# Differential attention: squares of the output rows ahead of two casts, and the third transposes of a step behind six products

## The chip, the core and the metric

The kernel runs on one core of a Trainium2 chip. What is measured is the device time of one execution in microseconds (us). Three runs of the kernel before have a median of 2905.68 us (2904.09 to 2906.51). The engines are named as in the profile: PE is the matrix engine (PEld its weight loads, which run beside its matmuls), DVE the vector engine, ACT the scalar (activation) engine, POOL the general engine, SP the engine that issues most DMAs (transfers between memory and the chip).

## What is computed

One layer of a hybrid model for two streams, a prompt of 256 tokens and 2048 latent tokens. The part that the change touches is differential attention with four heads: two softmax maps are formed from the same keys, the second is subtracted with a factor, and the result is multiplied with the values and normalised per row.

```python
def diff_attention(q, k, v, lam):
    ...
        s = jnp.einsum('bqhmd,bkhmd->bhmqk', qblk, k).astype(jnp.float32) * scale
        p = jax.nn.softmax(s, axis=-1)
        a = p[:, :, 0] - lam * p[:, :, 1]
        return jnp.einsum('bhqk,bkhe->bqhe', a.astype(v.dtype), v)
...
def merge(attn, four, subln_g, lam_init, w_out):
    b, n = attn.shape[:2]
    a = rms_norm(attn, subln_g) * (1.0 - lam_init)
    return jnp.concatenate([a.reshape(b, n, ATTN_WIDTH), four], axis=-1) @ w_out
```

The latent queries attend to 512 cached and 2048 new keys, 2560 in all. Projections, a Fourier mixing, the output projection and an MLP stand before and behind the attention; the change leaves them as they are.

## The kernel before

**Tiles.** For each of the 4 heads the 2048 latent queries are cut into 8 groups of 256, which makes 32 groups. A group has two halves j of 128 queries and two maps m. For each (j, m) there are five score blocks of 128 queries by 512 keys (`fill`, L1081, two matmuls each), a row maximum per block on DVE (`rowmax`, L1086), a combination of the five maxima (`comb`, L1089), and five exponentials on ACT (`exp`, L1105) that write the tile P0 (m = 0) or P1 (m = 1). POOL then forms P0 plus factor times P1 (`combine`, L1112 to L1121).

The 2560 keys are 20 tiles of 128, taken in pairs kb = 0, 2, ..., 18. For a pair, PE transposes four 128x128 pieces of P0 into one PSUM bank (`tr`, L1136, tile `pts`), ACT casts that bank into a high part (`ah`, L1143, tile `ahs`), DVE subtracts to get the low part (`al`, L1148, tile `als`), and PE multiplies both tiles of the pair with the values in three products each (`mul`, through `mm3`, L95 to L97). Pair 4 stays one whole fp32 copy and is multiplied by L1162. Pair 14 (tiles 14 and 15), like all the others, is split into two parts.

**PSUM.** It has eight banks: five for scores, two for `pts`, and one, `po`, which all groups share. In `po` columns 0 to 255 gather the products of a group. Columns 256 to 511 hold the finished group's output after it is transposed back (`o2`, L1177), from which ACT takes the squares and their row sums (`o4`, L1183, tile `osqs`). The `pts` banks alternate, so the transposes of a pair wait until `al` of the pair before the last one has read its bank.

**Order.** The attention's order is written out by hand: each call is entered with a due time in a list, which is then sorted, and each engine runs its share of that list in order. T is one step, u a fifth of it. A group's keys take four steps, with the pairs (0, 2), (4, 6, 8), (10, 12) and (14, 16, 18). A step also holds the scores, maxima and exponentials of a later group. In this document the four steps are called:

- **A**: transposes of 10 and 12, products of 4, 6, 8. The squares of the preceding group stand here.
- **B**: transposes of 14, 16, 18, products of 10 and 12.
- **C**: transposes of the next group's 0 and 2, products of 14, 16, 18.
- **D**: transposes of 4, 6, 8, products of 0 and 2. The preceding group's `o2` stands here.

In step A of a group, ACT's list reads: five exponentials into P0, the casts of 10 and 12, the two squares of the group before, then five exponentials into P1. PE's list reads: transposes of 10, three score blocks, transposes of 12, two score blocks, L1162 (pair 4), products of 6 and 8. In four of a head's eight cycles PE also has two small matmuls of the prompt stream (L1221) behind the products of step B, and in one cycle the prompt's products (L1256) in the middle of B.

The due times that the change edits, with w the start of a step (L1345) and, in L1355, of the output part of a group:

```python
tr_t, ah_t, al_t = [0.7, 2.2, 3.86], [3.2 if q == 3 else 3.3, 3.8, 4.4], [3.22 if q == 3 else None, 4.6, 5.2]
...
add(w + T + (3.9 + 0.01 * n) * u, gr.mul, kb)
...
for t, fn in ((0, gr.o1), (0.4, gr.o2), (7.85, gr.o4), (9.2, gr.o5), (11.8, gr.o6), (16.3, gr.o7), (23.4, gr.o8), (26.0, gr.o9)):
```

## Time and profile before

| what | us |
|---|---|
| median of three runs | 2905.68 |
| the profiled execution | 2906.36 |
| its span, first to last instruction | 2904.6 |
| PE busy | 2833.2 |
| DVE busy | 1995.9 |
| ACT busy | 1538.4 |
| POOL busy | 1073.8 |

The profile holds one execution. The attention runs from about 545 to 1292 us of the span. Read the whole first, then the stage: PE is busy for 98% of the span, but inside the attention less, and there DVE, ACT and POOL are each busy for four fifths of the time or more. In a row of the timeline stand the start in us, the duration in us (for merged rows the whole run of them), the engine, the line, the operation, the tile written and the tiles read, shapes, the count, and in brackets the idle time before it with what ended that. Ends of PE's matmuls are modelled. PE's granted clock is full in the attention.

### The profile page before, as it was taken

Reading aid. Unit: us, or ns where it says so; the run is one execution under the profiler, and the core shown is the slowest. Engines: PE = TensorE matmul, PEld = TensorE weight load, DVE = VectorE, ACT = ScalarE, POOL = GpSimd, SP = SyncE. Lnnn points to the kernel's source line nnn. Section 1 sums busy time; section 2 is a strip of 40 time slices with the busy share of each in tenths; the row PEclk is TensorE's granted clock in tenths of the full one; section 3 lists DMA queues with packets and bytes.
Section 4 is the critical chain, followed back from the end, with each engine's and each line's share of the span. In section 5 each row is a group of like instructions: output and inputs, shape, how many; then the busy total and the mean of one; then the engine's idle time right before and its main releaser. Section 6 shows DMA issues by size and latency. Waiting matters only on the chain.

```text
span 2904.6 us, 43029 instructions
## 1 busy us (share of the span) xinstructions
PE 2833.2 (98%) x15029; PEld 2441.0 (84%) x15029; DVE 1995.9 (69%) x3357; ACT 1538.4 (53%) x3479; POOL 1073.8 (37%) x887
## 2 busy tenths in 40 slices
PE   8999999999999999989999999999999999999999
PEld 5888888677777777778889999999998888888887
DVE  7767786888887888874468778777775354345554
ACT  4333333888888888863346556556554332232221
POOL 1211124788888888862213333333332000000000
PEclk9999999999999999999999999999999999999999
DMA  7776767332222321336786667676656454445663
GB/s 280 222 205 203 228 204 252 140 108 45 77 72 52 108 43 43 95 68 194 229 260 212 223 231 240 223 240 222 220 192 243 149 188 153 137 145 179 205 212 109
DMA packets 403707, 497.17 MB, mean 171 GB/s; under 512 B 31475, under 2 KB 319584, under 8 KB 400418
## 3 DMA queue, kind: packets, MB, share of 16 engines
q1 hardware_dynamic: 398000, 483.83, 52.7%
q0 software_dynamic: 1936, 7.41, 0.8%
q10 hardware_dynamic: 3554, 3.17, 0.3%
q8 instruction: 119, 1.95, 0.3%
q14 instruction: 98, 0.80, 0.1%
HBM read 316.78 MB, written 179.62 MB: 171 GB/s over the span
## 4 chain that ended last, share of the span: by engine, by line
PE 53%; DVE 1%; DMA 1%; ACT 0%; issue 0%; SPq 0%; POOL 0%; DVEq 0%
PE ps L95 8%; PE ps L97 8%; PE ps L96 8%; PE pC L1759 2%; PE pB L1760 2%; PE pB L1759 2%; PE pC L1761 2%; PE pC L1760 2%; PE pB L1761 2%; PE pA L1760 2%; PE pA L1761 2%; PE pA L1759 2%; PE po L97 2%; PE po L95 2%; PE po L96 2%; PE pD L1761 1%
## 5 line engine op out<-in xcount | busy, mean ns | idle before, releaser
L1086 DVE TENSOR_REDUCE mxs<-Ss 128x1 f32<-128x512 f32 x636 | 407.7, 685 | 123.6 <-PE Ss L1081 114.2
L1436 DVE TENSOR_TENSOR sl<-sr,sh 128x768 fp32r<-128x768 f32 x168 | 161.8, 964 | 331.5 <-ACT sh L1435 331.0
L1121 POOL TENSOR_TENSOR P0s<-P0s,P1s 128x1024 f32<-128x1024 f32 (+2 forms) x128 | 376.6, 2942 | 10.7
L1435 ACT CAST sh<-sr 128x768 fp32r<-128x768 f32 x168 | 140.6, 838 | 418.2 <-PE ps L96 418.2
L1801 POOL TENSOR_TENSOR gs<-g,g 128x384 f32<-128x384 f32 x48 | 69.8, 1453 | 469.6 <-ACT g L1771 426.4
L1105 ACT ACTIVATE P1s<-Ss,mxs 128x512 f32<-128x512 f32 x318 | 215.5, 694 | 35.4 <-DVE mxs L1089 34.1
L95 PE MATMUL pj<-wh,hh 128*128 128x512 f32 x576 | 228.3, 396 | 2.8 <-DVE hh L556 2.0
L96 PE MATMUL pj<-wl,hh 128*128 128x512 f32 x576 | 227.1, 394 | 0.5 <-DVE wl L517 0.5
L95 PE MATMUL ps<-thT,sh 128*128 128x512 f32 x585 | 227.6, 389 | 0.0
L96 PE MATMUL ps<-tlT,sh 128*128 128x512 f32 x585 | 227.6, 389 | 0.0
L97 PE MATMUL ps<-thT,sl 128*128 128x512 f32 x585 | 227.6, 389 | 0.0
L97 PE MATMUL pj<-wh,hl 128*128 128x512 f32 x576 | 225.5, 392 | 0.0
L1105 ACT ACTIVATE P0s<-Ss,mxs 128x512 f32<-128x512 f32 x318 | 214.6, 692 | 4.9 <-DVE mxs L1089 4.0
L1143 ACT CAST ahs<-pts 128x512 fp32r<-128x512 f32 x288 | 165.5, 607 | 81.5 <-PE pts L1136 81.4
L1136 PE MATMUL pts<-ident,P0s 128*128 128x128 f32 x1280 | 192.8, 274 | 15.1 <-DVE als L1148 11.8
L1136 PEld LDWEIGHTS pts<-ident,P0s 128*128 128x128 f32 x1280 | 148.6, 140 | 55.8 <-PE Ss L1081 25.7
L1148 DVE TENSOR_TENSOR als<-pts,ahs 128x512 fp32r<-128x512 f32 x288 | 185.3, 681 | 10.8 <-ACT ahs L1143 10.6
L1081 PE MATMUL Ss<-KS1s,Qs 128*128 128x512 f32 x636 | 190.1, 422 | 2.1 <-ACT P0s L1105 2.1
L1081 PE MATMUL Ss<-KS0s,Qs 128*128 128x512 f32 x636 | 189.3, 418 | 0.4 <-ACT P1s L1105 0.4
L1770 ACT ACTIVATE g<-uz 128x384 f32<-128x384 f32 x144 | 75.7, 526 | 200.2 <-DVE uz L1793 174.1
L1120 POOL TENSOR_SCALAR P1s<-P1s,tots 128x1024 f32<-128x1024 f32 (+2 forms) x128 | 172.0, 1344 | 5.7
L95 PE MATMUL po<-ahs,Vs 128*128 128x256 f32 x576 | 172.3, 299 | 0.0
(530 smaller groups left out, 8003.9 us busy)
## 6 DMA issues: line engine op xcount, KB each, us to landing
sr<-sd SPq DMA_DIRECT2D x84, 768.0 KB, 4.5
a<-in_w SPq DMA_DIRECT2D x184, 256.0 KB, 3.9
sd<-gs SPq DMA_DIRECT2D x192, 192.0 KB, 2.0
sd<-g SPq DMA_DIRECT2D x144, 192.0 KB, 2.0
wm<-in_w_mod SPq DMA_DIRECT2D x32, 512.0 KB, 5.6
Qs<-qd SPq DMA_DIRECT2D x32, 512.0 KB, 5.9
b<-in_w SPq DMA_DIRECT2D x64, 256.0 KB, 4.8
b<-tsum SPq DMA_DIRECT2D x64, 256.0 KB, 4.8
```

Of the source, the lines that this page charges most:

```text
L95: nc.tensor.matmul(ps, lh, rh, start=first, stop=False)
L96: nc.tensor.matmul(ps, lh, rl, start=False, stop=False)
L97: nc.tensor.matmul(ps, ll, rh, start=False, stop=last)
L1081: nc.tensor.matmul(S[:, :w], self.Q[:, x, m, j * P:j * P + P], self.hd.KS[m][:, b * 512:b * 512 + w], start=(x == 0), stop=(x == 1))
L1086: nc.vector.tensor_reduce(self.mx[j][:, m, b:b + 1], self.S[j, m, b], axis=AX.X, op=ALU.max)
L1105: nc.scalar.activation(dst, S, AF.Exp, bias=self.mx[j][:, m, 6:7], accum_out=self.sm[j][:, m, b:b + 1])
L1121: nc.gpsimd.tensor_add(d, d, p)
L1136: nc.tensor.transpose(pt[:, c:c + P], self.p0[j][:, (kb + t) * P:(kb + t + 1) * P], ident)
L1148: nc.vector.tensor_sub(t, self.pt[kb], f32(self.A[kb][0]))
L1759: nc.tensor.matmul(ps, wh[:, c], hh[:, k, :], start=first and k == 0, stop=False, skip_group_check=True)
L1760: nc.tensor.matmul(ps, wh[:, c], hl[:, k, :], start=False, stop=False, skip_group_check=True)
L1761: nc.tensor.matmul(ps, wl[:, c], hh[:, k, :], start=False, stop=k == 3, skip_group_check=True)
```

## The change

Two due times differ.

```diff
-                            tr_t, ah_t, al_t = [0.7, 2.2, 3.86], [3.2 if q == 3 else 3.3, 3.8, 4.4], [3.22 if q == 3 else None, 4.6, 5.2]
+                            tr_t, ah_t, al_t = [0.7, 2.2, 3.905 if q == 3 else 3.86], [3.2 if q == 3 else 3.3, 3.8, 4.4], [3.22 if q == 3 else None, 4.6, 5.2]
...
-                    for t, fn in ((0, gr.o1), (0.4, gr.o2), (7.85, gr.o4), (9.2, gr.o5), (11.8, gr.o6), (16.3, gr.o7), (23.4, gr.o8), (26.0, gr.o9)):
+                    for t, fn in ((0, gr.o1), (0.4, gr.o2), (6.9, gr.o4), (9.2, gr.o5), (11.8, gr.o6), (16.3, gr.o7), (23.4, gr.o8), (26.0, gr.o9)):
```

The later edit in the code is the earlier in the cycle. On ACT in step A (here group 1 casts its pairs 10 and 12, group 3 has its exponentials, and the squares `osqs_0` are of group 0) the order before is:

```order
L1105 ACTIVATE P0s_3_0_5905,sms_3_0_5844<-Ss_3_0_0_4_5877,mxs_3_0_5843 128x512
L1143 CAST ahs_1_10_5950<-pts_1_10_5913 128x512
L1143 CAST ahs_1_12_5955<-pts_1_12_5939 128x512
L1183 ACTIVATE osqs_0_5957,osss_0_5958<-po 128x128 x2
L1105 ACTIVATE P1s_3_0_0_5979,sms_3_0_5844<-Ss_3_0_1_0_5918,mxs_3_0_5843 128x512
```

And on ACT at the same place after the change:

```order
L1105 ACTIVATE P0s_3_0_5905,sms_3_0_5844<-Ss_3_0_0_4_5877,mxs_3_0_5843 128x512
L1183 ACTIVATE osqs_0_5949,osss_0_5950<-po 128x128 x2
L1143 CAST ahs_1_10_5954<-pts_1_10_5913 128x512
L1143 CAST ahs_1_12_5959<-pts_1_12_5939 128x512
L1105 ACTIVATE P1s_3_0_0_5979,sms_3_0_5844<-Ss_3_0_1_0_5918,mxs_3_0_5843 128x512
```

The two squares have moved ahead of the two casts; the number of instructions is the same.

The other edit is on PE in step B, shown here for group 1 (`pts_1_16`, `pts_1_18` are its transposes, `po` its products). Before:

```order
L1081 MATMUL Ss_3_1_0_4_6024<-KS0s_5257,Qs_3_5621 128x512 x2
L1136 MATMUL pts_1_18_6029<-ident,P0s_1_0_5425 128x128
L1136 MATMUL pts_1_18_6029<-ident,P0s_1_1_5493 128x128
L1136 MATMUL pts_1_18_6029<-ident,P0s_1_0_5425 128x128
L1136 MATMUL pts_1_18_6029<-ident,P0s_1_1_5493 128x128
L95 MATMUL po<-ahs_1_10_5950,Vs_5315 128x256
L96 MATMUL po<-als_1_10_5977,Vs_5315 128x256
L97 MATMUL po<-ahs_1_10_5950,Vs_5315 128x256
L95 MATMUL po<-ahs_1_10_5950,Vs_5315 128x256
L96 MATMUL po<-als_1_10_5977,Vs_5315 128x256
L97 MATMUL po<-ahs_1_10_5950,Vs_5315 128x256
L95 MATMUL po<-ahs_1_12_5955,Vs_5315 128x256
```

On PE at the same place after the change:

```order
L1081 MATMUL Ss_3_1_0_4_6024<-KS0s_5257,Qs_3_5621 128x512 x2
L95 MATMUL po<-ahs_1_10_5954,Vs_5315 128x256
L96 MATMUL po<-als_1_10_5977,Vs_5315 128x256
L97 MATMUL po<-ahs_1_10_5954,Vs_5315 128x256
L95 MATMUL po<-ahs_1_10_5954,Vs_5315 128x256
L96 MATMUL po<-als_1_10_5977,Vs_5315 128x256
L97 MATMUL po<-ahs_1_10_5954,Vs_5315 128x256
L1136 MATMUL pts_1_18_6036<-ident,P0s_1_0_5425 128x128
L1136 MATMUL pts_1_18_6036<-ident,P0s_1_1_5493 128x128
L1136 MATMUL pts_1_18_6036<-ident,P0s_1_0_5425 128x128
L1136 MATMUL pts_1_18_6036<-ident,P0s_1_1_5493 128x128
L95 MATMUL po<-ahs_1_12_5959,Vs_5315 128x256
```

The four transposes of pair 18 have moved behind the six products of pair 10. Both edits stand once in each of the 32 groups, except that the squares of the last group have a place of their own behind the loop, which stays. On DVE and POOL no row moves. On SP one store of an output tile (`att`, L1208) changes places with one load of input rows (L1576) at the end of the attention.

## The prediction

> **What bounds the kernel now.** First the page, then the windows, then the list of waits. Over the span PE is the bound; in the attention it is not full.

> ```profile
> PE 2833.2 (98%) x15029; PEld 2441.0 (84%) x15029; DVE 1995.9 (69%) x3357; ACT 1538.4 (53%) x3479; POOL 1073.8 (37%) x887
> ```
> ```profile
> 560.00:1250.00 690.00, 653.13 (x4143) 536.42 (x4141) 564.78 (x1104) 586.04 (x1634) 596.00 (x472) 1.00 0.26 69
> ```

> In these 690 us PE is busy for 653.13 at the full granted clock (1.00), so 36.9 us are to be had there. The list of waits (engine, line, releaser: total us, times, longest) names two rows that hold nearly all of it:

> ```profile
> PE po L1162 <- ACT osqs L1183: 28.2, 31, 1.4
> PE pts L1136 <- DVE als L1148: 11.8, 27, 1.8
> ```

> The reader is to see that each edit aims at one of them. L1162 waits for the squares once in each cycle; the third transposes wait for a subtraction.

> I read one cycle engine by engine, steps A to C. PE:

> ```profile
> 724.39 1.18 PE L1081 MATMUL Ss<-KS1s,Qs 128*128 128x512 f32 x4
> 726.43 1.13 PE L1162 MATMUL po<-ahs,vf4s 128*128 128x256 f32 x4 [0.86 <-ACT osqs L1183]
> ...
> 728.82 0.60 PE L1136 MATMUL pts<-ident,P0s 128*128 128x128 f32 x4
> 729.17 1.63 PE L1081 MATMUL Ss<-KS0s,Qs 128*128 128x512 f32 x6
> 730.64 0.60 PE L1136 MATMUL pts<-ident,P0s 128*128 128x128 f32 x4
> 730.99 1.18 PE L1081 MATMUL Ss<-KS0s,Qs 128*128 128x512 f32 x4
> 732.55 0.63 PE L1136 MATMUL pts<-ident,P0s 128*128 128x128 f32 x4 [0.38 <-DVE als L1148]
> ...
> 733.26 0.28 PE L97 MATMUL po<-ahs,Vs 128*128 128x256 f32 x1
> ...
> 733.94 0.28 PE L97 MATMUL po<-ahs,Vs 128*128 128x256 f32 x1
> ...
> 734.54 0.63 PE L1136 MATMUL pts<-ident,P0s 128*128 128x128 f32 x4
> ```

> A cycle later L1162 starts and waits in the same way, 23.6 us on:

> ```profile
> 750.03 1.13 PE L1162 MATMUL po<-ahs,vf4s 128*128 128x256 f32 x4 [0.87 <-ACT osqs L1183]
> ```

> The stretch of ACT around the first of these two:

> ```profile
> 723.96 0.70 ACT L1105 ACTIVATE P0s<-Ss,mxs 128x512 f32<-128x512 f32 x1
> 724.53 0.22 ACT L1105 ACTIVATION_READ_ACCUMULATOR P0s<-Ss,mxs 128x1 f32 x1
> 724.62 1.09 ACT L1143 CAST ahs<-pts 128x512 fp32r<-128x512 f32 x2
> 725.57 0.32 ACT L1183 ACTIVATE osqs<-po 128x128 f32<-128x128 f32 x1
> ...
> 726.01 0.28 ACT L1183 ACTIVATE osqs<-po 128x128 f32<-128x128 f32 x1
> 726.19 0.19 ACT L1183 ACTIVATION_READ_ACCUMULATOR osqs<-po 128x1 f32 x1
> 726.71 0.69 ACT L1105 ACTIVATE P1s<-Ss,mxs 128x512 f32<-128x512 f32 x1 [0.33 <-DVE mxs L1089]
> ```

> **Edit 1, the squares first.** It adds no instruction. The squares start at 725.57 because two casts from 724.62 stand ahead; without these they start 0.95 earlier. L1162 starts 0.42 behind the second square's start (726.43 against 726.01), so its release moves to 725.06 + 0.42 = 725.48. When could PE use it? Its scores end at 724.39 + 1.18 = 725.57 as modelled, but work behind a score run starts 0.16 before that modelled end (730.64 against 729.17 + 1.63 = 730.80), so at 725.41. The release still comes last, by 0.07, and the gain is 726.43 - 725.48 = **0.95 us a cycle**. The other bound is the counted idle, 0.86; I take the first, since it is the time by which the late releaser moves.

> What is behind the moved work? The casts of 10 and 12 come later by the squares' 0.86 (two starts 0.44 apart, and as much again before the next instruction can go). Their readers, and those of step B, on DVE:

> ```profile
> 726.54 1.28 DVE L1148 TENSOR_TENSOR als<-pts,ahs 128x512 fp32r<-128x512 f32 x2
> 729.92 1.89 DVE L1086 TENSOR_REDUCE mxs<-Ss 128x1 f32<-128x512 f32 x3 [2.11 <-PE Ss L1081]
> 731.73 0.68 DVE L1148 TENSOR_TENSOR als<-pts,ahs 128x512 fp32r<-128x512 f32 x1
> ...
> 733.63 0.16 DVE L1089 TENSOR_REDUCE mxs<-mxs 128x1 f32<-128x5 f32 x1
> 733.71 1.28 DVE L1148 TENSOR_TENSOR als<-pts,ahs 128x512 fp32r<-128x512 f32 x2
> ```

> Cast 10 now ends near 724.62 + 0.86 + 0.60 = 726.08, before its subtraction at 726.54; cast 12 ends near 726.55, before its own at about 727.14. ACT waits 0.33 for the maxima ahead of 726.71, and the squares and casts together are as long as before, so the exponentials into P1 do not move. In B, DVE idles 2.11 us for PE's scores, so it follows PE by the full 0.95. Its first subtraction then comes at 730.78 and needs the cast of 14, whose row, with the later ones of ACT, is here:

> ```profile
> 730.04 0.60 ACT L1143 CAST ahs<-pts 128x512 fp32r<-128x512 f32 x1
> ...
> 733.22 0.59 ACT L1143 CAST ahs<-pts 128x512 fp32r<-128x512 f32 x1 [1.36 <-PE pts L1136]
> ...
> 733.83 0.69 ACT L1105 ACTIVATE P0s<-Ss,mxs 128x512 f32<-128x512 f32 x1
> ...
> 735.37 0.34 POOL L1112 TENSOR_SCALAR tots<-tots,nlam 128x1 f32<-128x1 f32 x1 [2.10 <-ACT P0s L1105]
> ...
> 736.00 0.30 PEld L1081 LDWEIGHTS Ss<-KS1s,Qs 128*128 128x128 f32 x2 [0.34 <-ACT P0s L1105]
> ```

> That cast ends at 730.64: a margin of 0.14, the narrowest of the cycle. POOL idles 2.10 before C and keeps over 1 us.

> There are 31 such waits. 29 are of this kind: 29 x 0.95 = 27.6 us. The last two, at the end, are longer:

> ```profile
> 1268.73 1.03 PE L1136 MATMUL pts<-ident,P0s 128*128 128x128 f32 x8
> 1271.21 1.13 PE L1162 MATMUL po<-ahs,vf4s 128*128 128x256 f32 x4 [1.45 <-ACT osqs L1183]
> ...
> 1284.76 1.13 PE L1162 MATMUL po<-ahs,vf4s 128*128 128x256 f32 x4 [1.40 <-ACT osqs L1183]
> ```

> There no exponentials stand directly ahead, and the squares can run while PE transposes 10 and 12. I take both waits whole: 2.8 us. **Edit 1: -30.4 us.**

> [...] The squares read columns 256 to 511 of `po` and L1162 writes columns 0 to 255: no byte in common, yet the row above shows 0.86 us of waiting. [...] Guarding by address would make the releaser in the list a wrong one, and edit 1 worth nothing.

> **Edit 2, the third transposes behind six products.** In B the scores could hand over at 730.99 + 1.18 - 0.16 = 732.01; the transposes start at 732.55, 0.14 after the subtraction that frees their bank (731.73 + 0.68). Six products fill that gap: the rows at 733.26 and 733.94 lie six products apart, 0.68, so 0.70 with the start. The transposes then start at 732.71, 0.16 later than now, of which 0.02 to 0.03 return because they no longer stall between the first two (0.60 long, not 0.63). I take **0.14 later**.

> Does PE get its 0.38 back? The next bank is wanted at 734.54 for the transposes of step C, and that start stands 0.15 behind the second subtraction (733.71 + 0.68 = 734.39), which hangs on DVE's maxima and not on this order. So PE reaches it half a microsecond early and waits there: the wait moves, the step keeps its length.

> Who waits for the third cast? ACT idles 1.36 for it; it ends at 733.81 and the exponential starts at 733.83, when the maxima (733.63 + 0.16) are done too: both arrive together. 0.14 on the cast is 0.14 on the exponentials of C, and the weight load of the third score block there already waited 0.34 for them (736.00). From there PE has no idle until A that could absorb it. So edit 2 **costs** 0.14 in each of 27 cycles, 3.8 us. In one cycle per head the prompt's products stand in B and the transposes come later anyhow:

> ```profile
> 1064.84 1.18 PE L1081 MATMUL Ss<-KS0s,Qs 128*128 128x512 f32 x4
> 1066.12 0.63 PE L1136 MATMUL pts<-ident,P0s 128*128 128x128 f32 x4
> ```

> Scores hand over at 1065.86, plus 0.70 is 1066.56, against 1066.12: 0.44, less 0.03, in four cycles: 1.6 us. **Edit 2: +5.4 us**, between -11.8 (all of the wait in the list is saved) and +22 (31 x 0.70, the products whole); the rows above are nearest.

> The swap on SP puts a 512 KB load ahead of a store at the end of the attention. A load of that size, and PE behind that place:

> ```profile
> Qs<-qd SPq DMA_DIRECT2D x32, 512.0 KB, 5.9
> ```
> ```profile
> 1300.00:1400.00 100.00, 99.40 (x471) 82.70 (x470) 52.35 (x78) 33.90 (x84) 22.32 (x24) 1.00 0.72 213
> ```

> One landing, 5.9 us, bounds it on either side; with PE at 99.4% it is hidden, and I take nothing.

> **Sum** against the profiled execution of 2906.36 us: -30.4 + 5.4 = -25.0, so **2881.4**. That execution lies 0.7 above the median of the runs, within their spread.

> **The rivals.**

> - Edit 2 is free or a gain. For it: the wait is in the list, and 16 of the cycles have prompt matmuls ahead of the next bank, which take up some of the earliness. Against: cast and maxima end together. From 2876 (cost nothing) to 2870 (half of the 11.8 saved). 10%.
> - The next wait takes over. In B the margin of 0.14 between the cast of 14 and its subtraction decides: if squares and casts in the new order push the exponentials into P1 by more than that, DVE, the second subtraction and the next bank slip. 0.3 to 0.4 a cycle gives back 9 to 12: 2890 to 2893. Against it: 0.33 of idle on ACT. 11%.
> - Squares behind an exponential start late. The only idle behind a square is the 0.33 before the exponential; if it were a cost of changing function and fell due at the squares, edit 1 loses 29 x 0.33 = 9.6: 2891. 3%. [...]
> - Slower, and the change not doing what it says. If L1162 is held by something else that came just before the squares, edit 1 is worth nothing and edit 2's later cast is left: 2906.4 + 5.4 = 2912, up to 2928. It decides as soon as edit 1 gives less than 5.4 / 31 = 0.17 a cycle. Against it: without the two long ones the waits are (28.2 - 2.85) / 29 = 0.87 each, as even as a fixed order behind the squares would make them. 4%.

> **How the numbers follow.** Forecast 72%, rivals 10, 11, 3 and 4%. The range runs from 2873, where edit 2 is free with a little of its wait saved, to 2891, where the next wait or the late squares begin to give back. About 0.2% (5.8 us) is what a measurement can tell from no change. All cases but the last are faster by more: faster 0.95, same 0.02, slower 0.03.

> **What would show it.** Edit 1: the wait of L1162 for the squares falls from 28.2 us to below 4, and L1162 starts come 22.7 to 22.9 us apart, not 23.6. Edit 2: the third transposes wait for nothing; the first transposes of C wait some 0.3 to 0.5 for a subtraction instead; ACT idles longer before the third cast; PE's score blocks in C show waits for exponentials. If the cycle is under 22.65, edit 2 was free; if the subtraction of 14 waits for its cast, the margin was the step that failed; if the cycle is still 23.6, edit 1 was.

## The result and the profile after

The changed kernel takes 2876.74 us (median of 4 runs, 2873.97 to 2878.94), the kernel before, run beside it, 2905.02 us. The ratio is 0.9902, with a 95% interval of 0.9885 to 0.9919. The profiled execution took 2876.21 us, its span is 2874.4. The forecast was 2881.4 with a range of 2873 to 2891.

The first part of the page of the changed kernel (engine, busy time, share of the span, instructions), and its windows over the attention without the first and last microseconds (length, busy time of PE, PEld, DVE, ACT and POOL, granted clock, DMA share, GB/s):

```profile
PE 2832.3 (99%) x15029; PEld 2445.7 (85%) x15029; DVE 1995.9 (69%) x3357; ACT 1531.6 (53%) x3479; POOL 1074.6 (37%) x887
```
```profile
560.00:1225.00 665.00, 651.98 (x4146) 540.16 (x4145) 565.97 (x1106) 581.16 (x1638) 597.57 (x473) 1.00 0.28 71
```

PE's work is the same; its idle time in these windows is 13.0 us here and was 36.9. Four rows of the changed kernel's list of waits say what went:

```profile
PE pts L1136 <- DVE als L1148: 10.7, 27, 1.8
PEld po L1162 <- ACT osqs L1183: 10.1, 31, 0.3
PE Ss L1081 <- ACT P0s L1105: 1.9, 5, 1.1
ACT ahs L1143 <- PE pts L1136: 58.0, 71, 2.1
```

PE has no row for L1162 any more (28.2 us before). Only the weight load that runs ahead of it still meets the squares, 0.3 us each, beside other matmuls. The wait for the subtraction L1148 has nearly kept its size (11.8 before). One cycle of the changed kernel shows that it is another wait under the same name; the timelines of PE, ACT and DVE, cut to the lines in question:

```profile
718.54 1.13 PE L1162 MATMUL po<-ahs,vf4s 128*128 128x256 f32 x4
...
724.83 0.60 PE L1136 MATMUL pts<-ident,P0s 128*128 128x128 f32 x4
...
726.65 0.63 PE L1136 MATMUL pts<-ident,P0s 128*128 128x128 f32 x4 [0.51 <-DVE als L1148]
```
```profile
718.12 0.28 ACT L1183 ACTIVATE osqs<-po 128x128 f32<-128x128 f32 x1
...
718.38 1.06 ACT L1143 CAST ahs<-pts 128x512 fp32r<-128x512 f32 x2
719.79 0.69 ACT L1105 ACTIVATE P1s<-Ss,mxs 128x512 f32<-128x512 f32 x1 [0.34 <-DVE mxs L1089]
...
725.46 0.59 ACT L1143 CAST ahs<-pts 128x512 fp32r<-128x512 f32 x1 [1.25 <-PE pts L1136]
725.95 0.69 ACT L1105 ACTIVATE P0s<-Ss,mxs 128x512 f32<-128x512 f32 x1
```
```profile
723.84 0.68 DVE L1148 TENSOR_TENSOR als<-pts,ahs 128x512 fp32r<-128x512 f32 x1
...
725.75 0.16 DVE L1089 TENSOR_REDUCE mxs<-mxs 128x1 f32<-128x5 f32 x1
```

The row at 724.83 is the third transposes of step B: no wait (0.38 before). The row at 726.65 is the first transposes of step C: they now wait 0.51. The other cycles show the same: the first transposes of the next group wait 0.51 to 0.53, or 0.25 to 0.29 where PE comes to them later, mostly because the two small prompt matmuls (L1221) stand ahead (0.41 in the first cycle). L1162 starts 22.56 to 22.63 us apart in the ordinary cycles (those without the prompt's work; one or two stray by 0.3), against 23.54 to 23.60 before. From the first L1162 to the last it is 695.95 us (557.89 to 1253.84), against 725.75: -29.8. Ahead of the first the changed kernel is 1.1 us shorter, which no edit touches (over the twelve profiles of this document the first L1162 lies between 556.3 and 559.7 us). From the start of the last L1162 to the end of the span it is 0.8 us longer (1620.6 against 1619.8). Together that is, but for rounding, the 30.15 us between the two profiled executions.

### The profile page after: what moved, and what is told of

It is laid out like the page before. It is cut to its first block, busy times and chain, and to the rows that moved or that the text cites. A ratio compares the mean times of both kernels' runs of the same rounds, so it can differ in the third digit from the quotient of the medians.

```text
span 2874.4 us, 43052 instructions
## 1 busy us (share of the span) xinstructions
PE 2832.3 (99%) x15029; PEld 2445.7 (85%) x15029; DVE 1995.9 (69%) x3357; ACT 1531.6 (53%) x3479; POOL 1074.6 (37%) x887
## 4 chain that ended last, share of the span: by engine, by line
PE 53%; DVE 1%; DMA 1%; ACT 0%; issue 0%; POOL 0%; DVEq 0%; SPq 0%
PE ps L95 8%; PE ps L96 8%; PE ps L97 8%; PE pB L1761 2%; PE pB L1759 2%; PE pB L1760 2%; PE pC L1759 2%; PE pA L1759 2%; PE pC L1761 2%; PE pA L1761 2%; PE pA L1760 2%; PE pC L1760 2%; PE po L97 2%; PE po L96 2%; PE po L95 2%; PE pD L1759 1%
## 5 line engine op out<-in xcount | busy, mean ns | idle before, releaser
L1086 DVE TENSOR_REDUCE mxs<-Ss 128x1 f32<-128x512 f32 x636 | 407.8, 686 | 97.0 <-PE Ss L1081 85.7
L1105 ACT ACTIVATE P1s<-Ss,mxs 128x512 f32<-128x512 f32 x318 | 215.2, 694 | 36.2 <-DVE mxs L1089 32.8
L97 PE MATMUL ps<-thT,sl 128*128 128x512 f32 x585 | 227.6, 389 | 0.0
L97 PE MATMUL pj<-wh,hl 128*128 128x512 f32 x576 | 225.6, 392 | 0.0
L1105 ACT ACTIVATE P0s<-Ss,mxs 128x512 f32<-128x512 f32 x318 | 214.6, 694 | 4.2 <-DVE mxs L1089 4.0
L1136 PE MATMUL pts<-ident,P0s 128*128 128x128 f32 x1280 | 193.1, 274 | 13.6 <-DVE als L1148 10.7
L1081 PE MATMUL Ss<-KS1s,Qs 128*128 128x512 f32 x636 | 192.9, 425 | 1.9 <-ACT P0s L1105 1.9
L1143 ACT CAST ahs<-pts 128x512 fp32r<-128x512 f32 x288 | 162.7, 606 | 58.3 <-PE pts L1136 58.0
L1148 DVE TENSOR_TENSOR als<-pts,ahs 128x512 fp32r<-128x512 f32 x288 | 185.5, 681 | 8.5 <-ACT ahs L1143 8.4
L1081 PE MATMUL Ss<-KS0s,Qs 128*128 128x512 f32 x636 | 189.6, 418 | 0.4 <-ACT P1s L1105 0.4
L1136 PEld LDWEIGHTS pts<-ident,P0s 128*128 128x128 f32 x1280 | 149.4, 140 | 45.4 <-issue 9.1
## 6 DMA issues: line engine op xcount, KB each, us to landing
wm<-in_w_mod SPq DMA_DIRECT2D x32, 512.0 KB, 5.3
Qs<-qd SPq DMA_DIRECT2D x32, 512.0 KB, 6.3
```

Of the source, the lines that this page charges most:

```text
L97: nc.tensor.matmul(ps, ll, rh, start=False, stop=last)
L1081: nc.tensor.matmul(S[:, :w], self.Q[:, x, m, j * P:j * P + P], self.hd.KS[m][:, b * 512:b * 512 + w], start=(x == 0), stop=(x == 1))
L1086: nc.vector.tensor_reduce(self.mx[j][:, m, b:b + 1], self.S[j, m, b], axis=AX.X, op=ALU.max)
L1105: nc.scalar.activation(dst, S, AF.Exp, bias=self.mx[j][:, m, 6:7], accum_out=self.sm[j][:, m, b:b + 1])
L1136: nc.tensor.transpose(pt[:, c:c + P], self.p0[j][:, (kb + t) * P:(kb + t + 1) * P], ident)
L1148: nc.vector.tensor_sub(t, self.pt[kb], f32(self.A[kb][0]))
```

## Experiments

Two theories of why the change beat its forecast stood at the start: edit 2 costs less than its 5.4 us, or edit 1 gives more than its 30.4. The first two kernels do one edit each. Every ratio is against the kernel before on the same chip.

**Edit 1 alone.**

```diff
-for t, fn in (..., (7.85, gr.o4), ...):
+for t, fn in (..., (6.9, gr.o4), ...):
```

> Edit 1 alone: the squares stand ahead of the casts of 10 and 12, the third transposes stay where they were. Both edits together took 28.3 us off the median (2905.0 to 2876.7). Theory: edit 2 is worth nothing within 1.5 us, because the exponentials of step C follow the maxima and not the third cast; then this runs at 2875 to 2878, L1162 starts 22.6 us apart in most cycles, and the third transposes still wait 0.4 to 0.5 for a subtraction. Rival, the working of the prediction: edit 2 costs 5.4 us, so without it 2871. Second rival: edit 2 saved its wait, so without it 2882 to 2888.

Measured: 2875.78 us (2875.11 to 2879.37; ratio 0.9899, 0.9884 to 0.9914). Ordinary cycles are 22.56 to 22.62, as in the changed kernel, and the third transposes wait as before:

```profile
723.11 0.63 PE L1136 MATMUL pts<-ident,P0s 128*128 128x128 f32 x4 [0.38 <-DVE als L1148]
```

First to last L1162 takes 694.5 us, 31.3 less than before. Edit 1 alone does all that the change does. The first theory held.

**Edit 2 alone.**

```diff
-tr_t, ah_t, al_t = [0.7, 2.2, 3.86], ...
+tr_t, ah_t, al_t = [0.7, 2.2, 3.905 if q == 3 else 3.86], ...
```

> Edit 2 alone: the third transposes stand behind the products of 10, the squares stay behind the casts. Theory (edit 2 worth nothing): 2904 to 2907, cycles of 23.6 us, the wait of L1162 for the squares 28 us as before, the wait for the subtraction moved from the third transposes to the first transposes of the next group. Working of the prediction: 2910. Rival that it saves its wait: 2893 to 2900.

Measured: 2907.5 us (2905.92 to 2909.97; ratio 1.0004, 0.9996 to 1.0013), just above the upper expectation. L1162 waits 28.1 us for the squares, as before. The ordinary cycles are 23.54 to 23.61, unchanged. The four cycles with the prompt's products take 24.85 to 24.89 instead of 24.58 to 24.62. First to last L1162 is 1.6 us longer, 1.1 of it in these four.

**The third transposes behind both pairs of products**, with edit 1. If a later third cast is free at every size, this is free too; if it is free only up to a margin, the rest shows in full.

```diff
-[0.7, 2.2, 3.905 if q == 3 else 3.86]
+[0.7, 2.2, 3.915 if q == 3 else 3.86]
```

> Both edits, but the third transposes behind the products of 10 and of 12, so 0.70 us later still. Theory: the third cast had about no slack left against the maxima (its successor starts 0.1 us before it ends); 0.70 more makes it the last to arrive, the exponentials of C start 0.6 to 0.7 later, and the third score block with them: cycles of 23.2 to 23.3 us, 2893 to 2899. Rival: the exponentials hang on the maxima alone and the third cast is free to move: 2876 to 2878.

Measured: 2899.43 us (2897.59 to 2901.65; ratio 0.9977, 0.9968 to 0.9987), cycles 23.24 to 23.30. ACT and DVE in one of its cycles:

```profile
708.15 0.59 ACT L1143 CAST ahs<-pts 128x512 fp32r<-128x512 f32 x1 [1.89 <-PE pts L1136]
708.63 0.69 ACT L1105 ACTIVATE P0s<-Ss,mxs 128x512 f32<-128x512 f32 x1
```
```profile
707.76 0.16 DVE L1089 TENSOR_REDUCE mxs<-mxs 128x1 f32<-128x5 f32 x1
```

Here the maxima are done at 707.92 and the exponential starts at 708.63: the cast holds it. It starts 0.48 behind the start of the cast, 0.11 before the cast's listed end. In the changed kernel the maxima end at 725.91 and the exponential starts 0.04 behind them, 0.49 behind the start of the cast and 0.10 before its listed end. So in these traces the exponential needs the maxima plus 0.04 and the cast's start plus 0.48. In all twelve profiles no exponential behind a third cast starts earlier than these two, to within 0.01. In the kernel before, cast and exponential started 0.61 apart (733.22 and 733.83): the cast had 0.13 in hand. Edit 2 used that up and, outside the four cycles with the prompt's products, no more. Another 0.7 us of products then cost about 0.68 a cycle.

**The squares between the two casts**, with edit 2: half of edit 1.

```diff
-(7.85, gr.o4)
+(7.6, gr.o4)
```

> Both edits, but the squares between the casts of 10 and 12, half way back. Theory: L1162 is released by the squares, so one cast of 0.47 us ahead of them costs 0.40 to 0.47 a cycle in 29 cycles: cycles of 23.0 to 23.1 us, 2888 to 2891, and a wait of L1162 of 0.3 to 0.4 each. Rival: something that came just before the squares holds L1162: 2877 still. Second rival: any cast ahead brings the whole wait back: 2905.

Measured: 2898.14 us (2891.54 to 2900.33; ratio 0.9968, 0.9956 to 0.998). The cycles came as expected, 23.05 to 23.11, and so did L1162's wait:

```profile
PE po L1162 <- ACT osqs L1183: 13.0, 31, 1.0
```

Each cast ahead of the squares is half a microsecond a cycle. The total is 7 us above the expectation (the five runs lie between 2891.54 and 2900.33). In the profiled execution, 2896.35 us, 5.4 lie behind the last L1162 (1625.2 us to the end of the span, against 1619.8 before); up to 1.7 of that, an estimate of the last section, is a second dip of the granted clock (0.81 and 0.76 in two windows of 4 us from 1289.34). The kernel with the third transposes behind both pairs shows 1624.2 there, edit 1 alone 1622.9. This is where the next three runs look.

**The squares behind the products of 6 and 8**, with edit 2. The order on ACT and on PE is that of edit 2 alone; only who waits for whom changes.

```diff
-(7.85, gr.o4)
+(7.95, gr.o4)
```

> The third transposes as in the change, the squares a little later than in the kernel before, behind the issue of the products of 6 and 8, so that ACT's and PE's orders are those of the kernel with the transposes alone (2907.5), but the squares, which read columns 256 to 511 of po, come behind products that write columns 0 to 255, and the products no longer wait for the squares. No byte is shared. If a bank is guarded as one (what made L1162 wait): the squares wait for the products of 6 and 8, ACT stands until these are through, and exponentials, maxima and scores behind it slip: cycles near 25.4, 2945 to 2965. If guarded by address: no waits either way, the order of ACT as before and PE free of the squares: cycles 22.6 to 22.9, 2876 to 2886.

Measured: 2923.99 us in one run, so without an interval; cycles near 24.33. The list of waits of ACT, and ACT and PE in one cycle:

```profile
ACT osqs L1183 <- PE po L97: 54.7, 26, 2.1
```
```profile
704.86 0.28 PE L97 MATMUL po<-ahs,Vs 128*128 128x256 f32 x1
```
```profile
705.23 0.28 ACT L1183 ACTIVATE osqs<-po 128x128 f32<-128x128 f32 x1 [2.22 <-POOL P0s L1121]
```

The squares wait for the last product, which ends at 705.14, though they read other columns of `po`. (The single row names POOL as releaser; the list, over 26 cycles, names the products.) The wait between products and squares goes both ways, as the program sets it: L1162 waited 0.86 us for the squares in a cycle of the kernel before, and here the squares wait 2.1 us for the products. What the chip would do without the wait was not tried. The cost was overstated: some 0.75 a cycle against the kernel before, not 1.8. That L1162 no longer waits (0.95 of PE's time) would account for most of the difference; this is argued and not shown.

**Behind the attention: SP's order.** The cast of the second mix tile (`mh`, L1588 on DVE) waits for two loads on SP, L1581 and L1582. They stand behind the broadcast load L1199 of the seventh query group, which waits for that group's squares, a power on POOL and a store through memory. SP in the kernel before and in the changed one, and DVE in the changed one and in the kernel with edit 1 alone:

```profile
1292.07 0.32 SPq L1199 DMA_DIRECT2D rbs<-rs  x1
1292.44 0.43 SPq L1581 DMA_DIRECT2D mT<-att  x1
```
```profile
1263.85 0.32 SPq L1199 DMA_DIRECT2D rbs<-rs  x1
1264.22 0.43 SPq L1581 DMA_DIRECT2D mT<-att  x1
```
```profile
1270.63 0.69 DVE L1588 CAST mh<-mT 128x1024 fp32r<-128x1024 f32 x1 [1.36 <-DMA mT<-att]
```
```profile
1269.45 0.69 DVE L1588 CAST mh<-mT 128x1024 fp32r<-128x1024 f32 x1 [2.93 <-issue]
```

Before, the load goes out 7.7 us behind the start of the last L1162 (1284.76), in the changed kernel 10.4 us behind it (1253.84). PE is through the last two groups 2.5 us sooner, while the chain through POOL and memory has kept its length. With edit 1 alone the row names no releaser ("issue"); that it waits for the loads too is what the next kernel tests. That kernel has edit 1 and puts the two loads ahead of that group's broadcast load and store, whose DMA is taken out of `o7` into `o7b`:

```diff
+gr.late = h == H - 1 and g == 6
 if gr.last and t > 1:
     LASTO.append(fn)
+elif gr.late and t > 20:
+    LATE += [gr.o7b, fn] if t < 25 else [fn]
...
 mix_load(s1)
+for fn in LATE:
+    fn()
```

> The kernel with edit 1 alone (squares first, 2875.78), and at the end of the attention SP issues the two loads of the second mix tile (mT from att and from four) ahead of the broadcast load and the store of the last but one query group, which wait for POOL and for a round trip through memory. Theory (behind the attention the kernel pays for where SP's blocking entries stand, 0 to 4 us): the loads go out some 3 us earlier, the gap of 2.93 us ahead of the second cast into mh goes to under 0.3, PE's waits for mh fall from 4.3 to 1.7, and the time from the last L1162 to the end falls from 1622.1 to 1619.0 to 1619.5, so 2872.7 to 2873.2. Rival (the gap is the DMA transfer itself or another reader comes last, such as the weight splits): unchanged, 2875 to 2877. Second rival (the moved broadcast load now makes POOL, and by it the last stores, late): 2876 to 2880.

(This text and the next count the rest to some 0.7 us before the span's end; figures outside them go to its end.) Measured: 2877.72 us (2877.33 to 2878.74; ratio 0.9905, 0.9889 to 0.9922). The wait for `mh` went (0.2 us are left), as the first theory said, and the time did not, as the second rival said. The rest is 1622.6. The added lines shift the numbers: L1618, L1212 and L1216 below are L1607, L1204 and L1208 of the kernel before. PE at the first normalised tile, and DVE's list of waits:

```profile
1288.93 1.09 PE L249 MATMUL ptb<-ident,xn 128*128 128x128 f32 x8 [2.24 <-DVE xn L236]
```
```profile
DVE gt L1618 <- DMA g<-gate: 3.5, 2, 2.8
```

The gates stood behind the late store, and their wait took the place of the one removed. A dip of the granted clock (0.65 in the 4 us from 1288.97) followed PE's wait at L249, one dip more behind the attention than with edit 1 alone; so up to 1.7 us of what the move did not gain is the clock.

**The same move in the kernel with the third transposes behind both pairs.**

> The same move of SP's entries in the kernel whose third transposes stand behind both products (2899.43, gap ahead of the second mh 4.37 us, rest behind the last L1162 1623.44). Theory: the gap goes, the rest falls to 1619.0 to 1619.6, cycles stay at 23.24 to 23.30, and the time is 2895.0 to 2896.5; a larger gain than in the kernel with the squares alone, since the gap there was larger. Rival: unchanged, 2898 to 2901.

Measured: 2895.86 us (2894.43 to 2897.21; ratio 0.9966, 0.9955 to 0.9978), 3.6 less than without the move, and in the expected range. The rest fell by 4.9 us to 1619.3. Up to 3.4 us of that is the granted clock, which shows no dip here (1.00 in every window of 4 us from 1274.80 to 1338.80) and two without the move (0.84 and 0.73 in the two windows from 1281.45, 0.62 and 0.95 in the two from 1293.45; last section). One of the two stood behind the wait for `mh` that the move removed; the other behind a wait of 1.73 us that both kernels have. So the 3.6 is not the load's alone.

**Gates and inputs ahead too**: the loop over `LATE` moves behind the gates' loads, with edit 1 alone and with the whole change.

```diff
 gate_load(g1[s], 0, s)
+for fn in LATE:
+    fn()
```

> The squares alone, as in the run with the loads of the second mix tile first (2877.72), but now the loads of the two input tiles and of the two gates stand ahead of the late broadcast load and store too: SP's order is rs store, mT from att, mT from four, xo, xo, g, g, rbs, att. In that run PE's wait for mh went (4.3 to 1.7), but DVE waited 3.5 us for g, the transposes of the first normalised tile (L249) waited 2.2 instead of 0.6, and the rest behind the last L1162 stayed at 1622.6 (1622.9 with the squares alone, span less start). Theory (what is blocked behind the entries that wait for POOL is what costs): with the gates through, no wait for g, L249 waits 0.6 to 1.0, the rest is 1619.0 to 1620.5, and the time 2872 to 2875. Rival (POOL's chain of round trips for the last groups delays the first normalisation L92, which stands behind it): L249 waits 2 us or more still, 2876 to 2879. Beside both: after a pause of PE of about 2 us the granted clock has dipped to near 0.6 for some 4 us in most profiles, not in all; one dip is about 1.7 us either way.

> The same order of SP in the changed kernel (2876.74, rest 1620.6). Theory: its wait of 1.36 us for mT goes, the rest is 1619.0 to 1620.0, the cycles stay at 22.56 to 22.63 with 23.68 and 23.88, and the time is 2874.5 to 2876.5: a gain of 0.5 to 2, smaller than in the kernel with the squares alone. Rival (POOL's chain): 2877 to 2879.

Measured: 2876.80 us (2876.11 to 2877.07; ratio 0.990, 0.9885 to 0.9915) and 2877.61 us (2876.37 to 2879.27; ratio 0.9905, 0.9888 to 0.9921). The rival held in both. POOL and DVE of the first of them:

```profile
1288.57 0.58 POOL L1216 DMA_DIRECT2D att<-oTs  x1 [0.30 <-POOL oTs L1212]
1289.18 0.58 POOL L92 TENSOR_TENSOR nrsb<-nssb,mhalf 128x1 f32<-128x1 f32 x1
```
```profile
1289.79 0.75 DVE L236 TENSOR_SCALAR xn<-xo,nrsb 128x1024 f32<-128x1024 f32 x1 [3.10 <-POOL nrsb L92]
```

The normalisation L92 starts 0.03 behind the last group's store: it was queued behind that group's round trips. L249 on PE waits 3.0 us for it.

**And the normalisation ahead of the last group's multiplication and store on POOL**, with edit 1 alone:

```diff
-for fn in LASTO[2:]:
+for fn in LASTO[2:4]:
     fn()
...
 x_norm(s0)
+for fn in LASTO[4:]:
+    fn()
```

> The kernel with the squares alone and all loads ahead on SP (2876.80), and on POOL the first normalisation (L92, nrsb) now stands ahead of the last query group's multiplication and store. In the run before it stood behind them: the store ended at 1289.15, the normalisation started at 1289.18 though its input was there at 1286.68, DVE waited 3.10 us for it and the transposes L249 3.01. Theory (POOL's chain of round trips was what took the gain back): the normalisation starts near 1286.7, L249 waits 0.5 to 0.8, the rest behind the last L1162 falls from 1622.1 to 1619.4 to 1620.0, and the time to 2873.8 to 2875.0. Rival (yet another reader comes last behind the attention, such as the next mix tile's load, which stands behind the late store): L249 or the products wait about as long as before in sum, 2876 to 2878.

Measured: 2874.18 us (2873.72 to 2875.57; ratio 0.989, 0.9874 to 0.9907).

```profile
1286.04 0.57 POOL L92 TENSOR_TENSOR nrsb<-nssb,mhalf 128x1 f32<-128x1 f32 x1 [3.02 <-DVE nssb L230]
```
```profile
1287.92 1.09 PE L249 MATMUL ptb<-ident,xn 128*128 128x128 f32 x8 [1.12 <-DVE xn L236]
```

POOL now waits for its input and not the other way round, and L249's wait fell by 1.9 us. The time is in the expected range; L249 and the rest (1620.9) stayed somewhat above theirs. This is the lowest median of all, 2.6 us under the changed kernel, but the two intervals overlap, so it is not shown to be the faster.

## Why the prediction was right, and where it was off

**Edit 1: right.** The forecast was 0.95 us a cycle and 2.8 at the end, -30.4 in all. Measured with edit 1 alone: 1.3 and 1.2 at the two last waits (18.23 and 12.37 us against 19.54 and 13.55), -31.3 from first to last L1162, which leaves (31.3 - 2.5) / 29 = 0.99 a cycle. The release moved as reckoned: the second square starts at 718.12 and L1162 0.42 behind it. The narrow margin in B held: the subtraction of 14 (723.84) shows no wait.

**Edit 2: the mis-sized term.** The step that failed is the one that said of the third cast and the maxima "both arrive together", so that 0.14 on the cast is 0.14 on the exponentials of C. It compared the cast's listed end (733.81) with the exponential's start. The exponential needs only 0.48 behind the cast's start, so there were 0.13 in hand. The 3.8 us over 27 cycles were nothing (0.14 less 0.13). In the four prompt cycles the cast does hold the exponential, which starts 0.31 behind the maxima there: 0.41 less 0.13 is 0.28 a cycle, and the 1.6 came to 1.1. The 27 was a misreading besides: 26 of the listed waits are third transposes, one of 1.8 us at 550 us is not. Edit 2 as a whole costs some 1.5 us between the first and the last L1162 (694.5 without it, 695.95 with it) instead of 5.4. In the terms of the forecast this is the rival "edit 2 is free" without the saving, and its own sign, a cycle under 22.65, came. The forecast range of 2873 to 2891 holds this rival's 2876 too, so the measured total does not tell the two apart; the kernels with one edit do. The one with edit 2 does not differ from the kernel before by its interval.

The rest of what edit 2 was said to do came as said: the third transposes wait for nothing, the wait moves to the first transposes of C (0.51, against 0.3 to 0.5), and the step keeps its length. Two signs did not come. ACT's idle time before the third cast fell from 1.36 to 1.25: edit 2 alone raises it to 1.48, as said, but edit 1 alone lowers it to about 1.1, since ACT's work ahead of the cast then comes later against PE. And the score blocks of C have no new wait for the exponentials (5 times 1.9 us, 6 times 2.1 before).

**The end of the attention: not nothing.** The swap on SP was taken as hidden, bounded by 5.9 us. Behind the last L1162 the kernels differ from the kernel before by -0.5 to 5.4 us, of which up to 1.7 either way is one dip of the clock, and moving entries of SP's and POOL's queues moved waits there by 2 to 3 us. It is the place of entries that wait for a round trip, against a PE that arrives sooner, and not the swapped load by itself. For the change it comes to 0.8 us in one profile. How much of that is the swap was not separated.

**The sum.** Against the forecast's 2881.4 the profiled execution is 5.2 lower: 3.9 from edit 2, 0.9 from edit 1 and 1.1 ahead of the attention, less 0.8 behind it (the parts are rounded). The 1.1 ahead is chance.

## What to carry to other kernels

In these traces the listed end of a cast on ACT was not the time at which the exponential behind it could start: it started 0.10 and 0.11 us earlier. Read the smallest distance from start to start that the trace shows for the pair, and compare that with the other release before calling two arrivals equal. Here the waits that were removed brought PE through the last two groups 2.5 us sooner, but not the chain of small stores, round trips and broadcast loads that feeds what follows: the load behind it went out 10.4 us behind the last L1162 instead of 7.7. Look at what stands behind such entries on every queue. Where a wait reappears under the same name with the same total, look at which of the line's instructions has it.

## What the hardware showed unexpectedly

```profile
1293.55:1296.96 3.41, 1.84 (x6) 1.03 (x7) 3.38 (x5) 3.38 (x10) 0.83 (x1) 1.00 0.89 188
1296.96:1300.37 3.41, 3.41 (x10) 2.21 (x9) 3.41 (x6) 3.41 (x7) 2.42 (x4) 0.50 0.68 214
1300.37:1303.78 3.41, 3.41 (x16) 2.82 (x15) 3.31 (x5) 1.78 (x4) 0.00 (x0) 1.00 1.03 303
```
```profile
1280.60:1284.01 3.41, 2.10 (x15) 1.55 (x14) 1.31 (x2) 1.74 (x5) 0.59 (x1) 1.00 0.31 88
1284.01:1287.42 3.41, 2.06 (x7) 1.11 (x8) 3.38 (x6) 3.38 (x10) 0.00 (x0) 1.00 0.45 78
1287.42:1290.84 3.42, 3.42 (x17) 2.85 (x16) 3.42 (x6) 3.42 (x7) 0.72 (x1) 1.00 0.40 70
```

In the first, the wait (1292.92 to 1294.65) is followed by 3.41 us at a granted clock of 0.50, which costs 1.7 us of work (an estimate, half of the 3.41), and then by 1.00. In the second, the same wait (1283.17 to 1284.90) is followed by no dip. Of the twelve profiles ten show a dip there, and two (edit 1 alone and the one above) do not. A dip also followed a later wait of PE, 2.2 to 2.9 us long, in four kernels: edit 1 alone, the third transposes behind both pairs, the squares between the casts, and the two loads first. So the last three of these have two dips behind the attention.

The trace's record of the clock gives the times of the dips. In the kernel before they start at 34.03 and at 1296.96, 370 times 3.413 us apart; in the changed kernel at 33.53, 542.12 and 1265.74, the later two 149 and 361 times 3.413 us behind the first (all to within 0.13 us, and leaving out a dip at the very end of each record). Stretches of this length, counted from the first dip, are called steps here. Behind the attention each dip lasts one step (one lasts two, in the kernel with the squares behind the products: 0.73, 0.50 and 0.92 in three windows of 4 us from 1308.87). Ahead of the 14 dips in the 60 us behind the last L1162 of the twelve profiles, PE had 0.5 to 1.9 us of work in the step. No step at a granted clock of 1.00 with 2.0 us or more was followed by a dip there; four with 1.7 to 1.9 were not either. In the kernel without a dip the wait lies across two steps and leaves more than 2.0 us of work in each, and the waits of 3.0 and 3.2 us in the two kernels with the gates ahead, which leave 1.7 to 2.0 us in each of two steps, brought none. So in these profiles a wait came with a dip or without one mostly by where it fell in these steps. What else counts near 1.7 to 1.9 us stays open.

For this kernel it means that a wait of 1.7 us on PE can cost about twice its length (1.73 us of waiting and, by the estimate above, 1.7 us of work in the dip), and that single profiles of these kernels differ by a dip.
